# A two-block transformer kernel: the squares of the first input and their sums take a later place in the queues

## The chip, the cores and the metric

The kernel runs on one core of a Trainium2 chip. A core has five engines that run beside each other, each through its own queue in order: TensorE (PE) multiplies matrices into PSUM, VectorE (DVE) and ScalarE (ACT) work element by element, GpSimd (POOL) does small odd jobs, SyncE (SP) issues DMAs. They meet only in semaphores. The metric is the device time of one execution in microseconds (us), less is better; all times below are in us unless marked.

## The reference

One sequence of 512 tokens of width 1024 in float32 goes through two blocks. What the change touches is the beginning of the first:

```python
def rmsnorm(x, g):
    xf = x.astype(jnp.float32)
    y = xf * lax.rsqrt(jnp.mean(xf * xf, axis=-1, keepdims=True) + EPS)
    return (y * g.astype(jnp.float32)).astype(x.dtype)

xn = rmsnorm(h, norm_mix_g[l])
proj = xn @ w_in[l]
p = proj[..., :POOL_WIDTH]                       # 512 columns
uv = jax.nn.gelu(proj[..., POOL_WIDTH:], approximate=False)
u, v = uv[..., :SGU_WIDTH], uv[..., SGU_WIDTH:]  # 512 each
y_pool = pool_mixer(p, pool_w[l], pool_scale[l])
y_sgu = sgu_mixer(u, v, sgu_g[l], sgu_w[l], sgu_b[l])
h = h + jnp.concatenate([y_pool, y_sgu], axis=-1) @ w_out[l]
```

The rest of the first block is an attention over 256 memory tokens and a gated feed-forward with a convolution over three tokens. The second block has a strictly causal stick-breaking attention of 8 heads beside a depthwise convolution of 31 taps, and another such feed-forward:

```python
mask = s_idx < t_idx
log_beta = jax.nn.log_sigmoid(z)
log_one_minus = jnp.where(mask, jax.nn.log_sigmoid(-z), 0.0)
tail = lax.cumsum(log_one_minus, axis=3, reverse=True) - log_one_minus
weights = jnp.where(mask, jnp.exp(log_beta + tail), 0.0)
outs.append(jnp.einsum("bhqk,bkhd->bqhd", weights, vb))
```

## The kernel before

**Number format.** A float32 product is made of three matmuls (`mm3`, L122 to L125): each operand is split into a rounded upper part and a remainder (hi and lo), and hi x hi, hi x lo and lo x hi are added up in PSUM.

**Weights.** They come in units of 1 MB. `prep()` (L174) takes one: SyncE loads it into `raw`, ACT rounds it into `whi` (L195), DVE makes the remainder `wlo` (L196). Each of the three has two buffers. Unit 0 is loaded and rounded in five pieces (1, 1, 2, 2 and 2 eighths), in turn with the chunks of the input x (`load_x`), so that PE can begin early; later units are one piece. Ahead of each piece's rounding stands `first()`: it scales the x chunk with the norm's gain into `B` (ACT, L139) and the remainder `C` (DVE, L140). The norm's 1/rms is not in these: it is a number per token and is multiplied in behind the matmuls.

**The mean of squares.** `Stats.add` takes two chunks of x at a time: ACT squares them into a buffer t4 (L292; there are three of these buffers, shared with other work), DVE adds the halves into `acc` (L300 for the first pair, L303 and L304 for the others). `mean()` multiplies `acc` with ones on PE (L317, groups of four with one column each), POOL takes the power -1/2 (L325), giving `rc`, with one number per token. `spread()` makes from it a row for every partition: DVE L333, PE L336, ACT L338, giving `rb`.

**The first stage.** Units 0 and 1 (`sta_unit`, 48 matmuls each, into the PSUM pairs pp_190 and pp_279) make the pool mixer's 512 columns with the features on the partitions; DVE evacuates them times `rb` (L372), and the windowed sums follow. Then `mov_stage` makes v with the tokens on the partitions, from units 274 and 352 into the pairs pp_349 (tokens 0 to 255) and pp_350 (256 to 511), and ACT evacuates them by a Gelu with `rc` as its scale (L418). The PSUM pool has three pairs.

**Stick-breaking attention.** Per head pair and block of keys, scores z are made on PE (L774, L779), ACT does Abs, Exp and Ln (L782 to L784), DVE a maximum and sum (L785), giving log(1 - beta). It is split into hi (ACT, L131) and lo (DVE, L132), multiplied with -1 matrices on PE for the running sums (L798, L801), and ACT's Exp (L803) gives the weights, which are multiplied with v (L813). The convolution's taps (DVE, L832) are put between.

**What sets the order.** The program is written in one order, but each engine's queue is laid out by the tile framework's scheduler, which goes by a model of its own of each instruction's duration. `tc.issue_after(inst)` keeps what it wraps from being laid out before that instruction. As the scheduler is one pass over all the program, a constraint at the start can move instructions at a later place too.

Of the kernel before, what the change touches and what calls it, by code (L numbers as in the profile page):

```python
# [10 lines left out]
F32 = mybir.dt.float32  # L11
F32R = mybir.dt.float32r
AF = mybir.ActivationFunctionType
ALU = mybir.AluOpType
# [61 lines left out]
def block_kernel(  # L76
# [12 lines left out]
    pe, act, dve, pool, sp = nc.tensor, nc.scalar, nc.vector, nc.gpsimd, nc.sync  # L89
# [55 lines left out]
    def slot(name, dt=F32R, cols=2048):  # L145
        return slots.tile([P, cols], dt, tag=name, name=name)
# [18 lines left out]
    def whole(name, dt=F32R):  # L165
        return Chunks([slot(name + "0", dt), slot(name + "1", dt)])
# [5 lines left out]
    state = {"next": 0, "ready": [], "bank": 0}  # L172

    def prep(pieces=((0, 8),), before=None, between=None, early=None, slots=None):  # L174

        i = state["next"] if early is None else len(PLAN) + early
        if i == len(PLAN) and early is None:
            return
        if early is None:
            state["next"] += 1  # L180
        _, kind, place = (PLAN + EARLY)[i]
        n = place[2] * 256 if kind == "dwn" else UNIT
        raw = wp.tile([P, UNIT], F32, tag="raw", name="raw")
        hi = slot(slots[0]) if slots else wp.tile([P, UNIT], F32R, tag="whi", name="whi")
        lo = slot(slots[1]) if slots else wp.tile([P, UNIT], F32R, tag="wlo", name="wlo")
        for a, b in pieces:
            cs = slice(a * n // 8, b * n // 8)
            if before:
                before(a, b)
            sp.dma_start(out=raw[:, cs], in_=wts[i][:, cs])  # L190
        for a, b in pieces:
            cs = slice(a * n // 8, b * n // 8)
            if between:
                between(a, b)
            act.copy(hi[:, cs], raw[:, cs])  # L195
            dve.tensor_tensor(lo[:, cs], raw[:, cs], hi[:, cs].bitcast(F32), ALU.subtract)  # L196
        if kind == "hlf":
            views = tuple(w.rearrange("p (k j m) -> p k j m", k=4, j=4) for w in (hi, lo))
        elif kind == "mov":
            views = tuple(w.rearrange("p (k n) -> p k n", k=4) for w in (hi, lo))  # L200
        else:
            views = tuple(w[:, :n].rearrange("p (k j m) -> p k j m", j=2, m=P) for w in (hi, lo))
        if early is None:
            state["ready"].append(views)
        return views

    def weights():
        while len(state["ready"]) < 2 and state["next"] < len(PLAN):
            prep()
        return state["ready"].pop(0)  # L210
# [35 lines left out]
    h = whole("A", F32)  # L246
# [97 lines left out]
    st = Stats(eng=dve)  # L344

    def first(a, b):
        for j in range(a, b):
            scale_split(xh[:, j, :], xl[:, j, :], h[:, j, :], par("g_mix", j))

    prep(PIECES, load_x, first)  # L350
    sp.dma_start(out=sm[:, NFIRST:], in_=small[:, NFIRST:])
    prep()
    memr = half("D0", KC, M, F32)
    sp.dma_start(out=memr, in_=memT.rearrange("(c p) t -> p c t", p=P))
# [2 lines left out]
    sp.dma_start(out=sgw, in_=sguw.rearrange("s (h t) -> s h t", h=4))  # L357
    sp.dma_start(out=plw, in_=poolw.rearrange("c (g d) -> c g d", g=4))
    sp.dma_start(out=sgb, in_=sgub.rearrange("o (h t) -> o h t", h=4).to_broadcast([P, 4, P]))
    for c in range(4):  # L360
        st.add(h[:, 2 * c : 2 * c + 2, :], last=c == 3)

    dh, dl = half("E0", 4, T), half("E1", 4, T)
    for u in range(2):
# [119 lines left out]
    def residual(xh, xl, nxt_h, nxt_l, g, nk=KC):  # L484

        st = Stats()
        for u in range(4):
            pt = sta_unit(xh, xl, nk)
            hu = h[:, 2 * u : 2 * u + 2, :]
            dve.tensor_tensor(hu, pt, hu, ALU.add)  # L490
            for c in (2 * u, 2 * u + 1):
                scale_split(nxt_h[:, c, :], nxt_l[:, c, :], h[:, c, :], par(g, c))
            st.add(hu, last=u == 3)
        return st

    x2h, x2l = whole("F"), whole("G")
    st = residual(yh, yl, x2h, x2l, "g_x")
# [96 lines left out]
    st = residual(oh, ol, x3h, x3l, "g_ffn")  # L594
# [386 lines left out]
    st = Stats()  # L981
# [121 lines left out]
```

## Time and profile before

| | |
|---|---|
| median of 3 runs | 1246.66 (1246.56 to 1247.7) |
| profiled execution | 1246.8 |
| its span | 1245.1 |
| PE busy | 1226.2 (98%) |
| DVE busy | 771.2 (62%) |
| ACT busy | 485.2 (39%) |
| POOL busy | 110.0 (9%) |
| HBM read and written | 117.45 MB, 94 GB/s over the span |

The profiled execution is 0.14 above the median. A row of the timeline has the start, the length, the engine, the line of the kernel, the operation with what it writes and reads, the shapes and the count of neighbours taken together; in brackets stands the idle time of the engine before it and what ended it. Matmul lengths overlap: one of 512 columns is shown with 0.39, and the next one starts 0.227 later.

### The profile page before, as it was taken

What the parts mean: (1) busy time and instruction counts of PE and PEld (TensorE: products, weight loads), DVE (VectorE), ACT (ScalarE), POOL (GpSimd) and SP (SyncE); (2) the same over time, 40 slices, a digit from 0 to 9 for tenths busy, and PEclk for the clock granted to TensorE, in tenths of its full rate; (3) what the DMA queues carried; (4) which work ended last, traced back from release to release, by engine and by line L of the source; (5) the groups of instructions that cost most, each with busy time, mean ns of one, the idle gap of its engine ahead of it and who ended that gap; (6) DMA issues with size and microseconds to landing.
All of it is one profiled execution on the core that took longest, in us unless ns stands there. A gap on an engine that the chain in (4) does not pass through costs nothing.

```text
span 1245.1 us, 13634 instructions
## 1 busy us (share of the span) xinstructions
PE 1226.2 (98%) x5712; PEld 1009.9 (81%) x5712; DVE 771.2 (62%) x813; ACT 485.2 (39%) x528; POOL 110.0 (9%) x125
## 2 busy tenths in 40 slices
PE   8999999999999999999999899999999999999998
PEld 6889888788888888888888778677888888888887
DVE  7855634744766664466375999985775555346532
ACT  6433424623544342243254125873443333223310
POOL 1100210012000000000054412000400000000000
PEclk9999999999999999999999999999999999999999
DMA  8233332312222222222343012201222233223222
GB/s 275 97 106 131 102 102 68 136 68 101 74 97 102 102 102 102 92 83 97 118 152 135 0 35 68 68 1 68 102 99 81 92 102 102 102 102 102 84 68 86
DMA packets 20445, 118.32 MB, mean 95 GB/s; under 512 B 2208, under 2 KB 4128, under 8 KB 7712
## 3 DMA queue, kind: packets, MB, share of 16 engines
q1 hardware_dynamic: 20096, 117.20, 27.4%
q8 instruction: 44, 0.72, 0.2%
q10 hardware_dynamic: 288, 0.26, 0.1%
q14 instruction: 17, 0.14, 0.0%
HBM read 115.35 MB, written 2.10 MB: 94 GB/s over the span
## 4 chain that ended last, share of the span: by engine, by line
PE 92%; DVE 4%; ACT 2%; issue 1%; POOL 1%; DMA 0%; SPq 0%; DVEq 0%; ACTq 0%
PE pp L125 28%; PE pp L123 28%; PE pp L124 28%; DVE H L832 2%; PE ps L123 1%; PE ps L124 1%; PE ps L125 1%; POOL col L739 0%; PE ps L317 0%; DMA A<-in_xT 0%; PE ps L813 0%; DVE t L785 0%; PE pp L774 0%; ACT t L783 0%; PE pp L745 0%
## 5 line engine op out<-in xcount | busy, mean ns | idle before, releaser
L195 ACT CAST whi<-raw 128x2048 fp32r<-128x2048 f32 (+3 forms) x109 | 197.9, 1817 | 425.7 <-PE pp L124 358.5
L196 DVE TENSOR_TENSOR wlo<-raw,whi 128x2048 fp32r<-128x2048 f32 (+3 forms) x109 | 236.7, 2173 | 71.3 <-ACT whi L195 70.7
L123 PE MATMUL pp<-B,whi 128*128 128x512 f32 x672 | 261.7, 390 | 2.4 <-ACT whi L195 2.4
L125 PE MATMUL pp<-B,wlo 128*128 128x512 f32 x672 | 262.1, 390 | 0.2
L124 PE MATMUL pp<-C,whi 128*128 128x512 f32 x672 | 261.8, 390 | 0.0
L124 PE MATMUL pp<-G,whi 128*128 128x512 f32 x448 | 175.1, 391 | 0.0
L125 PE MATMUL pp<-F,wlo 128*128 128x512 f32 x416 | 162.2, 390 | 0.0
L123 PE MATMUL pp<-F,whi 128*128 128x512 f32 x416 | 161.5, 389 | 0.0
L123 PEld LDWEIGHTS pp<-B,whi 128*128 128x128 f32 x672 | 126.2, 188 | 29.3 <-ACT whi L195 3.3
L125 PEld LDWEIGHTS pp<-B,wlo 128*128 128x128 f32 x672 | 126.1, 188 | 27.8 <-DVE wlo L196 1.5
L124 PEld LDWEIGHTS pp<-C,whi 128*128 128x128 f32 x672 | 126.2, 188 | 26.7 <-issue 0.5
L124 PEld LDWEIGHTS pp<-G,whi 128*128 128x128 f32 x448 | 84.1, 188 | 17.6 <-issue 0.2
L625 DVE TENSOR_TENSOR A<-pp,A 128x1024 f32<-128x1024 f32 x23 | 28.2, 1224 | 105.6 <-PE pp L125 105.6
L646 DVE SCALAR_TENSOR_TENSOR H<-H,sm,H 128x512 f32<-128x512 f32 x132 | 92.8, 746 | 0.7
L125 PEld LDWEIGHTS pp<-F,wlo 128*128 128x128 f32 x416 | 78.1, 188 | 16.4 <-issue 0.2
L123 PEld LDWEIGHTS pp<-F,whi 128*128 128x128 f32 x416 | 78.1, 188 | 16.4 <-issue 0.2
L832 DVE SCALAR_TENSOR_TENSOR H<-H,sm,H 128x512 f32<-128x512 f32 x120 | 90.2, 780 | 1.2
L651 DVE TENSOR_TENSOR H<-pp,rb 128x1024 f32<-128x1024 f32 x22 | 26.8, 1224 | 50.6 <-PE pp L125 44.4
L128 ACT ACTIVATE H<-H,sm 128x512 f32<-128x512 f32 x70 | 54.3, 808 | 7.5 <-DVE H L698 7.5
L997 DVE TENSOR_TENSOR H<-pp,rb 128x512 f32<-128x512 f32 x22 | 15.2, 691 | 60.9 <-PE pp L125 54.7
L123 PE MATMUL pp<-D,whi 128*128 128x512 f32 x112 | 43.6, 389 | 0.0
L124 PE MATMUL pp<-E,whi 128*128 128x512 f32 x112 | 43.6, 389 | 0.0
(293 smaller groups left out, 1797.9 us busy)
## 6 DMA issues: line engine op xcount, KB each, us to landing
raw<-in_wts SPq DMA_DIRECT2D x99, 1024.0 KB, 4.8
raw<-in_wts SPq DMA_DIRECT2D x8, 768.0 KB, 4.0
A<-in_xT SPq DMA_DIRECT2D x3, 512.0 KB, 6.8
out<-A SPq DMA_DIRECT2D x3, 512.0 KB, 2.8
D<-in_memT SPq DMA_DIRECT2D x1, 1024.0 KB, 10.7
raw<-in_wts SPq DMA_DIRECT2D x3, 256.0 KB, 7.0
A<-in_xT SPq DMA_DIRECT2D x2, 256.0 KB, 3.9
raw<-in_wts SPq DMA_DIRECT2D x2, 128.0 KB, 4.1
```

What stands on the lines that cost most here:

```text
L123: pe.matmul(out, wh, xh, start=start, stop=False, **kw)
L124: pe.matmul(out, wh, xl, start=False, stop=False, **kw)
L125: pe.matmul(out, wl, xh, start=False, stop=stop, **kw)
L128: act.activation(out, in_, AF.Identity, scale=scale, bias=bias)
L195: act.copy(hi[:, cs], raw[:, cs])
L196: dve.tensor_tensor(lo[:, cs], raw[:, cs], hi[:, cs].bitcast(F32), ALU.subtract)
L625: dve.tensor_tensor(hu, pt, hu, ALU.add)
L646: dve.scalar_tensor_tensor(dst, hs[:, k : k + 512], w(k), dst, ALU.mult, ALU.add)
L651: dve.tensor_tensor(hs[:, :, 2:], pt, over2(rb), ALU.mult)
L832: tap = dve.scalar_tensor_tensor(cv[:, i, :], cc[:, i, k : k + 512], par("dw_w", 4 * k + i), cv[:, i, :], ALU.mult, ALU.add)
L997: dve.tensor_tensor(hs[:, 2:514], pt[:, 0, :], rb, ALU.mult)
```

## The change

`prep()` remembers its last rounding and its last remainder. All four calls of `st.add` are wrapped, so that nothing of them is laid out before the last rounding of unit 0 (`first_hi`) nor before the remainder of unit 1 (`state["lo"]`, the latest `prep()` at that place). No instruction is added or removed. Behind the change the line numbers are up by 3.

```diff
--- before.py
+++ after.py
@@ -192,8 +192,8 @@
             cs = slice(a * n // 8, b * n // 8)
             if between:
                 between(a, b)
-            act.copy(hi[:, cs], raw[:, cs])
-            dve.tensor_tensor(lo[:, cs], raw[:, cs], hi[:, cs].bitcast(F32), ALU.subtract)
+            state["hi"] = act.copy(hi[:, cs], raw[:, cs])
+            state["lo"] = dve.tensor_tensor(lo[:, cs], raw[:, cs], hi[:, cs].bitcast(F32), ALU.subtract)
         if kind == "hlf":
             views = tuple(w.rearrange("p (k j m) -> p k j m", k=4, j=4) for w in (hi, lo))
         elif kind == "mov":
@@ -348,6 +348,7 @@
             scale_split(xh[:, j, :], xl[:, j, :], h[:, j, :], par("g_mix", j))
 
     prep(PIECES, load_x, first)
+    first_hi = state["hi"]
     sp.dma_start(out=sm[:, NFIRST:], in_=small[:, NFIRST:])
     prep()
     memr = half("D0", KC, M, F32)
@@ -357,8 +358,10 @@
     sp.dma_start(out=sgw, in_=sguw.rearrange("s (h t) -> s h t", h=4))
     sp.dma_start(out=plw, in_=poolw.rearrange("c (g d) -> c g d", g=4))
     sp.dma_start(out=sgb, in_=sgub.rearrange("o (h t) -> o h t", h=4).to_broadcast([P, 4, P]))
+
     for c in range(4):
-        st.add(h[:, 2 * c : 2 * c + 2, :], last=c == 3)
+        with tc.issue_after(first_hi.ins), tc.issue_after(state["lo"].ins):
+            st.add(h[:, 2 * c : 2 * c + 2, :], last=c == 3)
 
     dh, dl = half("E0", 4, T), half("E1", 4, T)
     for u in range(2):
```

Where it goes, by the queues. First ACT in the first stage, before: `t4_*` are the squares, `whi_121` is unit 0, `whi_161` unit 1, `B` and `A` the scaled and the plain input.

```order
L195 CAST whi_121<-raw_120 128x512
L139 ACTIVATE B1_117<-A1_77,sm_73 128x512 x2
L292 ACTIVATE t4_180<-A1_77 128x1024
L195 CAST whi_121<-raw_120 128x512
L139 ACTIVATE B1_117<-A1_77,sm_73 128x512 x2
L292 ACTIVATE t4_184<-A1_77 128x1024
L195 CAST whi_121<-raw_120 128x512
L195 CAST whi_161<-raw_160 128x2048
L139 ACTIVATE H0_462<-D0_166,sm_73 128x256 x8
```

and in the changed kernel:

```order
L195 CAST whi_121<-raw_120 128x512
L139 ACTIVATE B1_117<-A1_77,sm_73 128x512 x2
L195 CAST whi_121<-raw_120 128x512
L292 ACTIVATE t4_172<-A0_76 128x1024
L292 ACTIVATE t4_176<-A0_76 128x1024
L292 ACTIVATE t4_180<-A1_77 128x1024
L195 CAST whi_161<-raw_160 128x2048
L139 ACTIVATE H0_462<-D0_166,sm_73 128x256 x8
L131 CAST G1_461<-G0_168 128x512 x2
L292 ACTIVATE t4_184<-A1_77 128x1024
L195 CAST whi_274<-raw_273 128x2048
L195 CAST whi_352<-raw_351 128x2048
L421 ACTIVATE F0_459<-pp_349,rc1_246 128x512 x2
```

Every square has left unit 0; three stand as a block ahead of unit 1's rounding, the fourth behind the memory's scaling (H0) and before unit 274's. The Gelu of pp_349 now stands ahead of the copy of `rb`.

Next PE in the first stage, as a difference: `acc_174` are the summed squares, pp_279 is unit 1's product, pp_349 and pp_350 the two token tiles.

```order
-L317 MATMUL ps0_239<-ones_83,acc_174 128x1 x4
 L125 MATMUL pp_279<-B0_116,wlo_162 128x512
...
-L336 MATMUL ps1_250<-t2_248,ones_83 128x512
 L124 MATMUL pp_279<-C1_119,whi_161 128x512
...
+L125 MATMUL pp_349<-whi_274,C0_118 128x512
+L317 MATMUL ps0_239<-ones_83,acc_174 128x1 x4
+L123 MATMUL pp_349<-whi_352,B1_117 128x512
...
+L336 MATMUL ps1_250<-t2_248,ones_83 128x512
 L123 MATMUL pp_350<-whi_274,B0_116 128x512
```

The sums' matmuls go from the front of unit 1 into the middle of pp_349, the spread from the end of unit 1 to between pp_349 and pp_350, and these two, mixed before, now stand one after the other; pp_350 takes the buffer of pp_349.

Then ACT in the last round of the stick-breaking attention, before (t4_5448, t4_5485 and t4_5542 are three blocks of scores; C0_5228, B0_5267 and D1_5095 their rounded logarithms; C1 and E1 weights):

```order
L783 ACTIVATE t4_5448<-t4_5448 128x1024
L803 ACTIVATE C1_5243<-pp_5358 128x768
L784 ACTIVATE t4_5448<-t4_5448 128x1024
L803 ACTIVATE E1_5282<-pp_5423 128x768
L782 ACTIVATE t4_5485<-pp_5468 128x768
L131 CAST C0_5228<-t4_5448 128x1024
L783 ACTIVATE t4_5485<-t4_5485 128x768
L784 ACTIVATE t4_5485<-t4_5485 128x768
L782 ACTIVATE t4_5542<-pp_5533 128x768
L783 ACTIVATE t4_5542<-t4_5542 128x768
L784 ACTIVATE t4_5542<-t4_5542 128x768
L131 CAST B0_5267<-t4_5485 128x768
```

and in the changed kernel:

```order
L786 ACTIVATE t4_5448<-t4_5448 128x1024
L787 ACTIVATE t4_5448<-t4_5448 128x1024
L806 ACTIVATE C1_5243<-pp_5358 128x768
L131 CAST C0_5228<-t4_5448 128x1024
L806 ACTIVATE E1_5282<-pp_5423 128x768
L785 ACTIVATE t4_5485<-pp_5468 128x768
L786 ACTIVATE t4_5485<-t4_5485 128x768
L787 ACTIVATE t4_5485<-t4_5485 128x768
L131 CAST B0_5267<-t4_5485 128x768
L806 ACTIVATE C1_5243<-pp_5439 128x1024
L785 ACTIVATE t4_5542<-pp_5533 128x768
L786 ACTIVATE t4_5542<-t4_5542 128x768
```

The first step (Abs) of t4_5485 has moved behind the cast of C0_5228 and the Exp of E1_5282, and t4_5542 behind the cast of B0_5267. PE and DVE are laid out to match: on DVE four taps instead of one stand between the remainder of C0_5228 and t4_5485. SyncE's queue is the same.

## Rows read from the trace of the kernel before

**Rows 1.** The page's first line: each engine's busy time.

```profile
PE 1226.2 (98%) x5712; PEld 1009.9 (81%) x5712; DVE 771.2 (62%) x813; ACT 485.2 (39%) x528; POOL 110.0 (9%) x125
```

**Rows 2.** Busy time by windows of the span, granted clock and DMA share, three stretches.

```profile
5.88:21.14 15.26, 12.60 (x51) 8.81 (x50) 12.71 (x21) 13.28 (x20) 0.82 (x2) 1.00 1.03 374
...
33.83:55.62 21.79, 21.79 (x97) 18.02 (x96) 18.29 (x27) 9.19 (x10) 2.13 (x3) 1.00 0.29 97
813.50:841.60 28.10, 26.46 (x157) 18.95 (x156) 21.99 (x29) 19.43 (x24) 0.00 (x0) 1.00 0.00 1
```

**Rows 3.** PE timeline of the first stage: start, length, group, idle before.

```profile
12.02 0.50 PE L123 MATMUL pp<-B,whi 128*128 128x512 f32 x1 [0.71 <-ACT whi L195]
...
21.59 0.95 PE L317 MATMUL ps<-ones,acc 128*128 128x1 f32 x8
22.41 0.47 PE L125 MATMUL pp<-B,wlo 128*128 128x512 f32 x1
...
31.16 1.02 PE L336 MATMUL ps<-t,ones 128*128 128x512 f32 x2
```

**Rows 4.** ACT timeline of the first stage.

```profile
9.18 1.33 ACT L139 ACTIVATE B<-A,sm 128x512 fp32r<-128x512 f32 x2
...
11.36 0.60 ACT L195 CAST whi<-raw 128x512 fp32r<-128x512 f32 x1
...
15.81 1.04 ACT L292 ACTIVATE t<-A 128x1024 f32<-128x1024 f32 x1
16.76 2.42 ACT L195 CAST whi<-raw 128x512 fp32r<-128x512 f32 x2
...
54.46 2.63 ACT L418 ACTIVATE F<-pp,rc 128x512 f32<-128x512 f32 x4
```

**Rows 5.** DVE timeline of the first stage.

```profile
19.81 2.29 DVE L196 TENSOR_TENSOR wlo<-raw,whi 128x2048 fp32r<-128x2048 f32 x1
...
32.83 1.22 DVE L372 TENSOR_TENSOR t<-pp,rb 128x1024 f32<-128x1024 f32 x1 [3.12 <-ACT rb L338]
```

**Rows 6.** SyncE's DMA issues of an x chunk and of unit 1.

```profile
3.12 0.44 SPq L249 DMA_DIRECT2D A<-in_xT  x1
...
7.68 0.65 SPq L190 DMA_DIRECT2D raw<-in_wts  x1
```

**Rows 7.** DMA landings of those two issues, us after the issue.

```profile
A<-in_xT SPq DMA_DIRECT2D x1, 512.0 KB, 5.8
...
raw<-in_wts SPq DMA_DIRECT2D x1, 1024.0 KB, 9.0
```

**Rows 8.** ACT timeline of the last attention round.

```profile
814.24 0.80 ACT L803 ACTIVATE E<-pp 128x768 f32<-128x768 f32 x1
815.05 0.81 ACT L782 ACTIVATE t<-pp 128x768 f32<-128x768 f32 x1
815.86 1.05 ACT L131 CAST C<-t 128x1024 fp32r<-128x1024 f32 x1
...
820.89 0.81 ACT L131 CAST B<-t 128x768 fp32r<-128x768 f32 x1
```

**Rows 9.** DVE timeline of the last attention round.

```profile
814.61 1.22 DVE L785 SCALAR_TENSOR_TENSOR t<-pp,t 128x1024 f32<-128x1024 f32 x1
...
819.78 0.95 DVE L785 SCALAR_TENSOR_TENSOR t<-pp,t 128x768 f32<-128x768 f32 x1
```

**Rows 10.** Conv taps on DVE in the last attention round, grouped.

```profile
L832 DVE SCALAR_TENSOR_TENSOR H<-H,sm,H x17: 739/745/753, 810.2 to 830.7; 128x512 f32<-128x512 f32 x17
```

**Rows 11.** PE timeline of the last attention round.

```profile
818.20 0.44 PE L801 MATMUL pp<-C,negtri 128*128 128x512 f32 x1
819.25 0.50 PE L801 MATMUL pp<-C,negtri 128*128 128x512 f32 x1 [0.61 <-DVE C L132]
...
821.76 0.33 PE L798 MATMUL pp<-B,negone 128*128 128x128 f32 x1 [0.72 <-ACT B L131]
...
841.59 1.08 PE L813 MATMUL ps<-B,E 128*64 128x512 f32 x4
```

## The prediction

> **What bounds the kernel now.** I read the page first: TensorE (PE) is busy 1226.2 of 1245.1 us [rows 1], so an edit counts only where PE stands still, or is made to. The windows come next, since the share is a mean over stages. From 5.88 to 21.14 us PE is busy 12.60 of 15.26; from 33.83 to 55.62 without a break, 97 matmuls, so one follows another by 0.227; from 813.50 to 841.60, the last round of the second block's attention, 26.46 of 28.10 [rows 2]. The granted clock is 1.00 (the 2.4 GHz level) in all three, so PE's waits there cost their own length and no slower matmuls afterwards. Then the timelines of PE, ACT and DVE in these stretches, and last the DMA landings, which say how early anything can start.
>
> What the reader is to see at the start: unit 0 comes in pieces, and PE waits for ACT's rounding of a piece, 0.71 at 12.02 for the third [rows 3]. On ACT a square of 1.04 stands ahead of the rounding of each piece but the first (the last of the four at 15.81) [rows 4]. That is the loss the edit goes at.
>
> The profiled run took 1246.8, its span 1245.1, so 1.7 lie around the span; the median is 1246.66. I sum on the span and carry the difference to the median.
>
> **Unit 0: -1.48.** Without squares a piece's rounding waits only for its x chunks. For the third piece they are issued at 3.12 and land 5.8 later, at 8.92 [rows 6, 7]. B's two halves take 1.33, the cast 0.60 [rows 4]: ready by 10.8, against 12.02 now. 36 matmuls follow: 36 x 0.227 = 8.2, plus lower parts not yet there. Now these add 21.14 - 12.02 - 8.2 = 0.9; DVE is then rid of the sums as well and I take 0.7 (estimate: the first of the restarts stays, half of the rest goes). Unit 0 ends at 10.8 + 8.2 + 0.7 = 19.66 against 21.14. The fourth and fifth roundings are ready at 12.7 and 14.7, ahead of their matmuls.
>
> **Unit 1: +0.90, so that only -0.58 of it is left.** All squares that a buffer is free for (three) now stand ahead of unit 1's rounding, one block: 14.71 + 3 x 0.945 (start to start) = 17.54. Raw unit 1 was issued at 7.68 and landed 9.0 later, at 16.7 [rows 6, 7], so the rounding starts 0.84 after it could. The rounding and piece 4's together take 2.42, 0.51 of it piece 4's [rows 4]: it ends at 19.45 (before: 19.18). The lower part takes 2.29 [rows 5]: 21.78. PE reaches the first matmul that reads it, the third of unit 1, at 19.66 + 0.45 = 20.11, and goes on at 21.83. Before, that matmul ran at 22.41, behind the column sums. So 1.48 shrinks to 22.41 - 21.83 = 0.58.
>
> **Column sums: +0.90.** L317 runs from 21.59 and the next matmul at 22.41, itself 0.08 longer than 0.39 [rows 3]: 0.90. Before, it stood in front of the matmul that would have waited for the lower part until 19.81 + 2.29 = 22.10 at least [rows 5], and so was mostly paid by that wait. Now it stands in the middle of pp_349, where nothing is waited for, and its 0.90 is paid in full. The spread (L336) costs the same in either place: 1.02 for two passes [rows 3].
>
> **Token tiles: +0.85.** Before, pp_349 and pp_350 were mixed and both had buffers: pp_190 was evacuated at 32.83 [rows 5]. Now the scale 1/rms comes later, pp_190 and pp_279 are still held, and pp_350 takes pp_349's buffer, when both Gelus of pp_349 have read it. By the terms above pp_349 ends at 44.40. The group of four Gelus at 54.46 takes 2.63 [rows 4]: two take 1.36, 0.05 for starting, so PE goes on at 45.86. L336 fills the wait till 45.12 only: +0.73, and 0.12 for a matmul that starts after a wait (0.50 instead of 0.39 at 12.02 [rows 3]). The Trainium skill, "Perfetto Trace Analysis", section "Optimizing Tensor Performance", wants independent matmul groups to rotate through PSUM banks, so that one is evacuated beside the next one's matmuls. That speaks against this order, and the trace agrees as far as it goes: with two buffers there is no idle time between 33.83 and 55.62 [rows 2]. Where the rule was kept the stage would be 0.85 shorter.
>
> First stage: -0.58 + 0.90 + 0.85 = **+1.2**. The rest lies under matmuls. The fourth square and the deferred sums on DVE come before unit 2's parts, but these are ready at 30.2 (wanted 32.4) and those of whi_352 at 36.7 (wanted 38.7); the pool's evacuation, now behind the Gelu on ACT, is over by 53.5, for a PSUM buffer and a unit wanted at 56.9. Each queue on SP is as it was. If that cover failed, the nearest is the 2 us at 38.7: a DVE queue late by 3 would cost 1. Bounds of the stage: without L317's price and the buffer wait -0.6; with twice the buffer wait +2.0.
>
> **Last attention round: +2.6.** Between 60 and 810 us the order is unchanged, but in the last round the scheduler shifted ACT: t4_5485's Abs/Exp/Ln now stand behind the cast of C0_5228 and behind the Exp of E1_5282. Before, E1's Exp (814.24) and t4_5485's Abs (815.05) ran while DVE made t4_5448 (814.61, 1.22 long), and the cast followed at 815.86 [rows 8, 9]. Now ACT has nothing from 814.4 to 815.87, E1's Exp starts at 816.83 (2.6 later), and Abs, Exp, Ln of t4_5485 end at about 820.3. On DVE four conv taps of 0.745 [rows 10] stand ahead of t4_5485's subtraction, which starts at 821.37 instead of 819.78 [rows 9]; with its 0.95 the cast to B0_5267 starts at 822.36 against 820.89 [rows 8]. PE's waits, walked in its new order with these times: 0.93 (t4_5448's subtraction), 0.19 (C's lower part), 2.03 (B's cast), 0.73 (C1's Exp), 0.86 (t4_5542's subtraction), 0.72 (B1's Exp): 5.46. Those that go, start to start: 819.25 - 818.43 = 0.82, then 0.95 up to 821.76 [rows 11], and two short ones of 0.3 each: 2.4. Of the difference of 3.1 I give 0.5 back, since the new order changes less often between the attention's matmuls and those of the next weight unit, and the first one behind such a change takes up to 0.12 more: 2.6. The last gather (841.59 [rows 11]) would be at 844.2. Nothing behind it waits for ACT or DVE so closely that this is won back. Bounds: if all waits that I put here are hidden and the old ones go, -2.3; if the old restarts stay beside the new waits, +4.5. I take 2.6, since each wait stands on durations of rows at the same tiles.
>
> **Sum.** 1.2 + 2.6 = +3.8: the profiled run at 1250.6, the median at 1250.5.
>
> **Rivals.**
> A: the first stage's +1.2 alone; the shifted tail costs nothing. For it: ACT is busy 19.43 and DVE 21.99 of 28.10 there [rows 2], so both have room. Against: PE follows their chain within 1 us, at 819.25 and 821.76. Time: 1246.66 + 1.2 = 1247.9.
> B, the other side: faster. Unit 0's 1.48 is kept if PE isn't held at the third matmul of unit 1. That decides at 20.11: the lower part has to end before it, which takes a rounding that starts at 16.0, and raw lands at 16.7. And the tail's old waits of 0.82 and 0.95 would have to vanish without new ones, C's cast being ahead of t4_5485's Exp and Ln. Full: -1.48 + 0.90 - 1.77 = -2.4, 1244.3; with no L317 cost 1243.4.
> C: the edit does nothing to see. PE's idle time moves from unit 0 to unit 1, L317 falls into a wait, the tail stays: -0.6 to +0.6, about 1246.6.
> D: the tail costs more, since each late cast holds the next square of the chain: +4.5, together 1252.4.
>
> **Chances.** Forecast (1249.2 to 1251.6) 0.50, D 0.17, A 0.13, C 0.10, B 0.10. What can be told from no change is 0.2%, 2.5 us: slower begins at 1249.2, faster ends at 1244.2. Forecast and D make 0.67 slower, 0.03 of A's cases come out above the line: 0.70. A's and C's rest and B where only its first half comes true: 0.22 within. Faster 0.08. The range, 1247.0 to 1252.8, reaches down to A and up to D and leaves out C and B.
>
> **What would show it.** Right: no wait of PE over 1 us between 8 and 20; unit 0 ends near 19.7; a wait of 1.7 for wlo at the third matmul of unit 1; L317 at about 38.7; a wait of PE for the Gelu (ACT) of 0.7 at 45; the first matmul behind the token tiles 1.2 later, at 56.9; and in the round around 815 to 824 us a wait near 2 for the cast of B. Wrong: unit 1 without a wait, or the last gather of B less than 2 us later against the stage's own start.

## The result: slower, by twice the forecast

The changed kernel takes 1254.38 us (median of 5, 1249.85 to 1255.13) where the kernel before takes 1246.69 (5 runs, 1246.56 to 1247.7): 7.7 more, a ratio of 1.0055 with a 95% interval of 1.0036 to 1.0073. The forecast was 1250.5, in a range up to 1252.8. The direction held, the size didn't.

The page of the changed kernel's profiled run (1254.99) has at its head:

```profile
span 1253.3 us, 13627 instructions
PE 1232.1 (98%) x5712; PEld 1014.8 (81%) x5712; DVE 772.9 (62%) x813; ACT 485.3 (39%) x528; POOL 111.6 (9%) x125
```

The span grew by 8.2, PE's busy time by 5.9 [rows 1], with the same instructions. A wait is not busy time: matmuls have become slower somewhere, and that is the first thing to look for. The mean granted clock of the run is 0.992 (before: 0.997). Four of the five timed runs have 0.992 or 0.993; the fifth, 1249.85, has 0.997.

To see where the time goes I follow six marks that both orders have:

| mark on PE | before | changed | difference |
|---|---|---|---|
| third matmul of unit 1 | 22.41 | 22.23 | -0.18 |
| first matmul behind the token tiles | 55.62 | 57.20 | +1.58 |
| column sums of the last norm (L317 x16) | 666.48 | 668.02 | +1.54 |
| last transposes of the keys (L745, L748) | 759.81 | 762.28 | +2.47 |
| last gather of the attention round | 841.59 | 850.47 | +8.88 |
| last matmul of the program | 1241.05 | 1249.22 | +8.17 |

So there are four steps: +1.6 in the first stage, +0.9 between 668 and 762, where the order is the same, +6.4 in the last attention round (forecast 2.6), and -0.7 after it. The last of them belongs to the round: the queues differ behind it too, up to about 900 us, and the changed one has four of the next norm's column sums (L898, 0.43 at 850.04) ahead of the last gather, where the old one has all eight behind it. So round and rest together cost 5.7.

The first stage, PE of the changed kernel, in the columns of [rows 3]:

```profile
10.70 0.49 PE L123 MATMUL pp<-B,whi 128*128 128x512 f32 x1 [1.55 <-ACT whi L195]
...
22.23 0.50 PE L125 MATMUL pp<-B,wlo 128*128 128x512 f32 x1 [1.59 <-DVE wlo L196]
...
38.24 0.95 PE L317 MATMUL ps<-ones,acc 128*128 128x1 f32 x8
...
44.63 1.02 PE L336 MATMUL ps<-t,ones 128*128 128x512 f32 x2
46.21 0.50 PE L123 MATMUL pp<-whi,B 128*128 128x512 f32 x1 [0.56 <-ACT F L421]
...
57.20 0.39 PE L123 MATMUL pp<-B,whi 128*128 128x512 f32 x1
```

Unit 0 has waits of 1.55 and 0.20, where before it had 1.71 (at 9.33) and 0.71; then come those that were forecast: 1.59 for unit 1's lower part, the sums alone at 38.24, and 0.56 for the Gelu at the token tiles. ACT shows why unit 1 is late, as against [rows 4]:

```profile
13.36 1.34 ACT L139 ACTIVATE B<-A,sm 128x512 fp32r<-128x512 f32 x2 [0.70 <-DMA A<-in_xT]
...
15.11 2.95 ACT L292 ACTIVATE t<-A 128x1024 f32<-128x1024 f32 x3
17.97 1.89 ACT L195 CAST whi<-raw 128x2048 fp32r<-128x2048 f32 x1
...
44.89 1.27 ACT L421 ACTIVATE F<-pp,rc 128x512 f32<-128x512 f32 x2 [10.16 <-PE pp L125]
```

The three squares take 15.11 to 17.97, and unit 1's rounding begins behind them.

The last attention round on PE, to set beside [rows 11]:

```profile
817.04 0.91 PE L777 MATMUL pp<-G,F 64*128 64x256 f32 x12 [0.96 <-ACT C L806]
...
825.70 0.33 PE L801 MATMUL pp<-B,negone 128*128 128x128 f32 x1 [1.15 <-ACT B L131]
826.62 1.44 PE L816 MATMUL ps<-C,E 128*64 128x512 f32 x4 [0.60 <-ACT C L806]
...
834.98 0.80 PE L123 MATMUL pp<-G,whi 128*128 128x512 f32 x1
835.58 0.63 PE L124 MATMUL pp<-G,whi 128*128 128x512 f32 x1
...
837.60 0.39 PE L123 MATMUL pp<-G,whi 128*128 128x512 f32 x1
...
850.47 1.08 PE L816 MATMUL ps<-B,E 128*64 128x512 f32 x4
```

The waits are no longer than the sum had them: 1.15 for B's cast (2.03 in the sum) and 0.60 for C1's second Exp (0.73). The one of 0.96 at 817 is as long as the first in the sum (0.93), but it is another: it ends with ACT's Exp of C1 from pp_5358, which the new order puts behind the Ln of t4_5448, and the sum had the subtraction of t4_5448 on DVE. What the sum did not have is below them. From the gather of four at 826.62 on the matmuls are slow: it takes 1.44 (1.08 at the end of the list, the same operation), and the first matmuls of the next unit stand 0.42 to 0.60 apart where 0.227 is usual. In windows (the columns of [rows 2]; the granted clock is the third number from the end):

```profile
817.00:824.00 7.00, 6.91 (x50) 4.91 (x50) 6.86 (x10) 4.15 (x5) 0.00 (x0) 1.00 0.00 0
824.00:827.00 3.00, 1.25 (x7) 0.68 (x7) 2.96 (x4) 2.18 (x3) 0.00 (x0) 1.00 0.00 0
827.00:838.00 11.00, 10.95 (x43) 7.71 (x40) 7.82 (x11) 8.02 (x10) 0.00 (x0) 0.53 0.00 0
838.00:850.00 12.00, 12.00 (x59) 9.28 (x59) 5.19 (x8) 5.28 (x7) 0.00 (x0) 1.00 0.01 1
```

PE is busy 1.25 of the 3.00 us before 827, and then the granted clock is 0.50, its 1.2 GHz level, from 827.2 to 837.5; after that 1.00 again. In the same round of the kernel before it is 1.00 throughout [rows 2].

### The profile page after: what moved, and what is told of

Its sections match the earlier page's. It is cut to its first block, busy times and chain, and to the rows that moved or that the text cites. A ratio compares the mean times of both kernels' runs of the same rounds, so it can differ in the third digit from the quotient of the medians.

```text
span 1253.3 us, 13627 instructions
## 1 busy us (share of the span) xinstructions
PE 1232.1 (98%) x5712; PEld 1014.8 (81%) x5712; DVE 772.9 (62%) x813; ACT 485.3 (39%) x528; POOL 111.6 (9%) x125
## 4 chain that ended last, share of the span: by engine, by line
PE 91%; DVE 4%; ACT 2%; POOL 1%; DMA 1%; issue 0%; SPq 0%; DVEq 0%; ACTq 0%
PE pp L123 28%; PE pp L124 28%; PE pp L125 28%; DVE H L835 2%; PE ps L123 1%; PE ps L124 1%; PE ps L125 1%; DMA A<-in_xT 1%; PE ps L816 0%; POOL col L742 0%; PE ps L317 0%; PE pp L804 0%; PE pp L777 0%; DVE wlo L196 0%; DVE t L788 0%
```

## The experiments

Two theories and a third, before the first four runs. **Theory 1**: the round's waits were summed rightly, and the rest is the granted clock, which falls because of them. **Theory 2**: the waits themselves cost 6.4. **Theory 3**: the clock falls since the round begins later, whatever its order. To separate stage and round, a table of instructions is put at the end of the program; it holds a stretch of each queue to a given order, by edges that make no wait:

```python
ORDER = ("5477-5484 5523-5528 5534-5541 5505-5520 5565 ...", ...)   # by number as traced
    by = {i.name: i for i in nc.cur_bb.bb.instructions}
...
        for one, two in zip(names, names[1:]):
            tc.add_manual_dep(by[two], one, ..., reason="order")
```

**1. The changed stage, the round as before.** The table holds the round to the order of before.

> The changed first stage with the last attention round in the order of before. Theory 1 (the changed order of the round lets the granted clock fall, and that is most of the missing size): the round keeps 1.00 and takes as long as before; what is left is the first stage's 1.5 and, behind the normalised queries, a low clock that lasts longer (0.9): 1248.2 to 1249.2. Theory 2 (the round's new waits cost 6.4 by themselves, the clock is no cause): the same 1248.2 to 1249.2. Theory 3 (the later arrival at the round, not its order, makes the clock fall): a low clock in the round here too, 1251 or more.

Measured: 1248.83 against 1247.06 (ratio 1.0015, 1.0006 to 1.0024): +1.8. The round, in windows:

```profile
813.00:830.00 17.00, 15.35 (x111) 11.25 (x112) 16.79 (x23) 15.71 (x20) 0.00 (x0) 1.00 0.00 1
830.00:860.00 30.00, 30.00 (x137) 22.58 (x134) 19.16 (x27) 11.88 (x15) 1.01 (x1) 1.00 0.10 36
```

The clock is 1.00 all through, and from the keys' last transposes (761.38) to the last gather (843.19) it takes 81.8, as before (841.59 - 759.81 = 81.8). The round begins nearly as late as in the changed kernel (762.28) and nothing falls: theory 3 is out for the profiled run. Ten of the eleven runs lie between 1247.89 and 1249.58; one of 1250.76 has a mean clock of 0.994 and no trace, so where its clock was low isn't known (run 5 shows a place in the first stage).

**2. The stage as before, the changed round.** The same table the other way round.

> The first stage of before with the last attention round in the order of the changed kernel. Theory 1: some runs, most of them perhaps, with a low clock in the round and 1251 to 1253.5, the others at 1248.5 to 1249.5. Theory 2: 1253 in all runs, whatever the clock. Theory 3: no low clock in the round, about 1249.2 (the 2.6 of waits alone).

Measured: 1252.07 (1250.81 to 1253.99), ratio 1.0042 (1.0029 to 1.0055): +5.0. The profiled run, a stretch of 14 us in the round:

```profile
823.00:837.00 14.00, 13.35 (x46) 9.03 (x47) 9.97 (x12) 9.37 (x11) 0.00 (x0) 0.51 0.00 0
```

Almost the whole stretch is at half speed, though the round begins as early as before. The clock falls at 823.3, which is behind the wait for B's cast and ahead of the next one:

```profile
823.01 0.33 PE L819 MATMUL pp<-B,negone 128*128 128x128 f32 x1 [1.15 <-ACT B L152]
823.93 1.97 PE L834 MATMUL ps<-C,E 128*64 128x512 f32 x4 [0.60 <-ACT C L824]
```

```profile
821.90:823.30 1.40, 0.29 (x1) 0.19 (x1) 1.36 (x3) 1.17 (x2) 0.00 (x0) 1.00 0.00 0
823.40:823.90 0.50, 0.00 (x0) 0.00 (x0) 0.50 (x2) 0.50 (x2) 0.00 (x0) 0.50 0.00 0
```

So in this run the wait of 0.60 was not needed for the fall. In the five runs the mean clock goes from 0.992 (1253.99 and 1253.46) over 0.994 (1252.07 and 1251.31) to 0.995 (1250.81): the time falls as the clock rises, so the price is not one fixed number, which speaks for theory 1 and against 2. The second group that theory 1 had, 1248.5 to 1249.5, did not come.

**3. The waits filled.** The changed kernel, with matmuls in PE's three long waits: four into an idle bank, eleven that add zeros to the gather's sum.

```diff
+        if (hp, n) == (3, 0):
+            idle = single(0).rearrange("p (a b) -> p a b", a=4)
+            for _ in range(4):
+                pe.matmul(idle, negone, over2(negone, 4), start=True, stop=True)
...
+            for _ in range(11 if (hp, n) == (2, 2) else 0):
+                pe.matmul(o[:HD, P:]..., identr[:HD, HD:], negone[:HD]..., start=False, ...)
```

> The changed kernel with TensorE's three long waits in the round filled by matmuls whose results are dropped (4 into an idle PSUM bank) or are zeros added to a sum (11). Theory 1: the granted clock stays 1.00 and the last gather comes some 4 us earlier than in the changed kernel; median 1249.5 to 1251. Theory 2: filling a wait gives nothing back, 1254 to 1255. Theory 3: as theory 2, the clock falls wherever the round begins at that time.

Measured: 1251.29 (1250.42 to 1253.19) against 1247.06, ratio 1.0035 (1.0022 to 1.0047): +4.2, where the changed kernel has +7.7. PE in the round, with the fillers (L796 and L840), and the windows in which the changed kernel waited and was slow:

```profile
815.25 1.09 PE L796 MATMUL ps<-negone 128*128 128x512 f32 x4
...
823.81 1.45 PE L840 MATMUL ps<-negone,identr 64*64 64x384 f32 x7
825.18 0.33 PE L828 MATMUL pp<-B,negone 128*128 128x128 f32 x1
825.44 0.91 PE L840 MATMUL ps<-negone,identr 64*64 64x384 f32 x4
...
846.67 1.08 PE L847 MATMUL ps<-B,E 128*64 128x512 f32 x4
```

```profile
824.00:827.00 3.00, 3.00 (x16) 1.49 (x14) 2.96 (x5) 2.82 (x4) 0.00 (x0) 1.00 0.00 0
827.00:838.00 11.00, 10.03 (x57) 7.44 (x56) 8.96 (x12) 7.52 (x10) 0.00 (x0) 1.00 0.01 1
```

More work, and 3.1 us less time (3.5 by the differences to before, 7.7 and 4.2). The clock stays at 1.00 and the last gather is at 846.67 instead of 850.47. Theory 2 falls, theory 1 stands. And the difference to the first run, 1251.29 - 1248.83 = 2.5, is about what the changed round costs without the clock, where the forecast had 2.6. In the traces it is made up otherwise: from the keys' last transposes (761.61) to the last gather it takes 85.1, 3.3 more than in run 1, and 0.7 comes back behind the gather.

**4. The squares behind unit 1's rounding.** The round is as before. In the changed kernel the constraint on unit 1's remainder, a DVE instruction, shows in the sums on DVE alone: the squares on ACT still stand ahead of unit 1's rounding. Here they are held behind that rounding.

```diff
-        with tc.issue_after(first_hi.ins), tc.issue_after(state["lo"].ins):
+        with tc.issue_after(state["hi"].ins), tc.issue_after(state["lo"].ins):
```

> The squares behind unit 1's rounding instead of ahead of it (their sums behind its lower part as in the changed kernel), the round in the order of before. If the block of three squares ahead of unit 1's rounding is what takes back unit 0's gain, the third matmul of unit 1 runs near 21.0 instead of 22.2, and the first matmul behind the token tiles at 55.9 to 56.3 instead of 57.2: total 0.9 to 1.2 below the run with the changed stage alone. If unit 1's rounding waits for its data anyway, no difference from that run.

Measured: 1247.58, ratio 1.0006 (0.9996 to 1.0015), 1.25 less than run 1. PE of the stage:

```profile
20.69 0.50 PE L146 MATMUL pp<-B,wlo 128*128 128x512 f32 x1 [0.86 <-DVE wlo L217]
...
44.82 0.50 PE L144 MATMUL pp<-whi,B 128*128 128x512 f32 x1 [0.56 <-ACT F L442]
...
55.81 0.39 PE L144 MATMUL pp<-B,whi 128*128 128x512 f32 x1
```

The third matmul of unit 1 is at 20.69 instead of 22.23, and the stage ends at 55.81 instead of 57.20 (57.06 in run 1). The block of squares costs what was expected, 1.25; the 0.56 at the token tiles and the sums' 0.9 remain, and eat the gain.

**5. Which waits?** Run 3 without the four matmuls of the first wait.

> The changed kernel with only the second and the third of the round's three long waits filled (1.15 and 0.60, both after 824), by 11 matmuls that add zeros; the first wait (0.96 at 817) stays empty. If these two make the clock fall, it stays at 1.00 and the time is that of the run with all three filled, 1250.5 to 1251.5 (the changed kernel: 1254.4). If the first wait has a part in it, some runs fall: 1252 to 1254.5.

Measured: 1250.98 (1250.84 to 1252.72), ratio 1.0033 (1.002 to 1.0045): as run 3. The wait of 0.95 at 817.77 is there, the clock in the round is 1.00. So the first wait alone let nothing fall in these runs, and one or both of the waits after 824 matter; by run 2 the first of these can be enough without the second. The profiled run is the one of 1252.72. Its low clock lies from 715 to 725, a stretch that comes up below, and in the first stage, behind the wait for unit 1's lower part:

```profile
21.31 0.50 PE L147 MATMUL pp<-B,wlo 128*128 128x512 f32 x1 [1.59 <-DVE wlo L218]
```

```profile
22.20:25.60 3.40, 3.40 (x10) 2.62 (x9) 3.40 (x10) 3.40 (x5) 0.00 (x0) 0.50 0.96 371
```

The wait of 1.59 is in the changed kernel and in runs 1 and 3 too, and there the clock is 1.00 in this window. Here the stretch from that matmul to the first one behind the token tiles takes 36.58 (to 57.89) and in the changed kernel 34.97: 1.6 more, in one execution of four.

**6. A better stage.** Squares and sums directly behind unit 1's parts, L317 in the middle of unit 1, everything else in the order of before, by a table.

> All four squares and their sums directly behind unit 1's parts, the column sums (L317) in the middle of unit 1, all else in the order of before (the two token tiles mixed, the spread in its old place). Theory 1 (three terms make the stage's 1.6: the block ahead of unit 1's rounding, the sums at full price, the wait for a PSUM pair): without the first and the third, the third matmul of unit 1 runs near 20.9 (before 22.41), the sums cost 0.9, no wait at the token tiles, and the stage ends 0.4 to 0.7 earlier than before: 1246.2 to 1246.8. Rival (the squares cost the same wherever they stand): the stage ends with before or later, 1247.0 and up.

Measured: 1248.58, ratio 1.001 (1.0001 to 1.0019): a miss. PE:

```profile
20.89 0.50 PE L164 MATMUL pp<-B,wlo 128*128 128x512 f32 x1 [0.86 <-DVE wlo L235]
...
26.37 1.05 PE L356 MATMUL ps<-ones,acc 128*128 128x1 f32 x8 [0.65 <-DVE acc L343]
...
55.95 0.39 PE L162 MATMUL pp<-B,whi 128*128 128x512 f32 x1
```

The third matmul of unit 1 comes at 20.89 as expected, and nothing is waited for at the token tiles. But L317 stands too early and waits 0.65 for DVE's sums; with its price the stage ends at 55.95, 0.33 later than before. The other part of the loss, 1.4 in the profiled run, lies between the last norm's sums (666.83) and the keys' last transposes (761.54; before 666.48 and 759.81), in the stretch that the next run is about. The rival's number came out, for another reason than it gave.

**7. The kernel before, its own two longest waits filled.** If a wait costs its length and the slow work behind it, that must hold in the kernel before as well. At 714 PE waits for the normalised queries:

```profile
713.97 1.56 PE L745 MATMUL pp<-ident,D 128*128 128x128 f32 x8 [3.64 <-DVE D L741]
717.62 1.94 PE L745 MATMUL pp<-ident,D 128*128 128x128 f32 x8 [2.08 <-DVE D L741]
719.32 0.80 PE L123 MATMUL pp<-E,B 128*128 128x512 f32 x1
719.91 0.63 PE L124 MATMUL pp<-E,B 128*128 128x512 f32 x1
```

```diff
+            if name == "G":
...
+                for _ in range((15, 10)[i]):
+                    pe.matmul(idle, negone, over2(negone, 4), start=True, stop=True)
```

> The kernel before with the two longest waits of TensorE (3.64 at 710 and 2.08 at 716, for the normalised queries) filled by 15 and 10 matmuls into an idle PSUM bank. Theory 1 (what a wait costs is its length and, where the clock falls, the work behind it at half speed): the clock stays 1.00 between 710 and 725, the transposes behind the first wait take 1.04 instead of 1.56, the matmuls of 717.6 to 721.8 run at full speed: 1.8 to 2.4 less, 1244.7 to 1245.4. Theory 2 (the clock is no cause of lost time): no difference, 1247.0.

Measured: 1245.67 (11 runs, 1245.07 to 1247.81) against 1247.2 (27 runs), ratio 0.9988 (0.9979 to 0.9996): 1.5 less, where 1.8 to 2.4 were expected. PE:

```profile
709.77 3.56 PE L784 MATMUL ps<-negone 128*128 128x512 f32 x15
713.82 1.06 PE L788 MATMUL pp<-ident,D 128*128 128x128 f32 x8 [0.49 <-DVE D L778]
714.63 2.54 PE L784 MATMUL ps<-negone 128*128 128x512 f32 x10
717.47 1.06 PE L788 MATMUL pp<-ident,D 128*128 128x128 f32 x8 [0.29 <-DVE D L778]
719.17 0.50 PE L160 MATMUL pp<-E,B 128*128 128x512 f32 x1 [0.64 <-DVE t L730]
719.51 0.40 PE L161 MATMUL pp<-E,B 128*128 128x512 f32 x1
```

The transposes take 1.06 instead of 1.56 and 1.94, the matmuls behind them are 0.23 to 0.34 apart instead of 0.42 to 0.59. From the last norm's sums to the keys' last transposes this run takes 92.66 (666.08 to 758.74), the profiled run of before 93.33, that of the changed kernel 94.26: 0.7 to 1.6 are won, and not 2: now PE waits 0.64 for DVE at 719.17, which did not show behind the slow transposes.

**8. Runs 6 and 7 together.**

> The two before this together. If they are independent, their differences add up: 2.2 to 3.1 below before, 1244.0 to 1244.9.

Measured: 1246.6, ratio 0.9996 (0.9987 to 1.0005). It is 0.9 above run 7, and 2.0 under run 6. The expected 1244.0 to 1244.9 did not come, since run 6 had no gain to add: its 1.4 lost and run 7's 1.5 won make -0.1, and -0.6 is measured. The fastest version is run 7, 1.5 below the kernel before, where the changed one is 7.7 above it.

## Why the forecast was wrong

**The step that failed** stands in its first part: "The granted clock is 1.00 (the 2.4 GHz level) in all three, so PE's waits there cost their own length and no slower matmuls afterwards." The clock was read in the old order, and taken over into an order with other waits; there it fell to 0.50 from 827.2 to 837.5, a price for which the sum had no term. Runs 1 and 3 give the price: 7.7 = 1.8 (stage, run 1) + 2.5 (the round's waits, run 3 less run 1) + 3.4 (what is left, and what filling the waits takes back: 3.1 to 3.5). The one execution of the changed kernel with a mean clock of 0.997 agrees: it took 1249.85, 3.2 more than before, where the forecast was 3.8. It has no trace. None of the rivals held it; rival D had a larger price of the round, but from waits.

**Unit 0 and unit 1**: right in kind. (The sign that no wait of PE is over 1 us between 8 and 20 did not come: 1.55 at 10.70. But the third piece starts there, as the sum had it, at 10.8.) Unit 1's rounding does stand behind three squares and PE does wait for the lower part; the wait was forecast as 1.7 and is 1.59. The gain that stays was forecast as 0.58 and is 0.18 (22.41 - 22.23): ACT waited for the last x chunks until 13.36 (before, they had landed at 12.95), the squares began at 15.11 and not at 14.71, and unit 1 moved by the same 0.4.

**Column sums** (+0.90) and **token tiles** (+0.85): right. L317 runs at 38.24 (forecast 38.7), PE goes on at 46.21 after a wait of 0.56 and the spread. Stage: -0.18 + 0.90 + 0.85 = 1.57, measured 1.58 in the trace and 1.8 in run 1, forecast 1.2. The order of PE differs between 77 and 90 us as well, where the sum had it unchanged; the marks at 57 and 668 differ by the same 1.5 to 1.6, so that cost nothing.

**The round's waits**: the total fits (2.5 against 2.6), in part by luck. Of the 5.46 of waits, the changed kernel and run 3 show 3.7: 0.96 for an Exp that the sum did not name, 1.15 for B's cast (2.03), 0.60 for C1's Exp (0.73), and in run 3 0.31 for the last subtraction (0.86) and 0.66 for B1's Exp (0.72); none for C's lower part (0.19). And the forecast had 2.6 at the last gather and nothing won back behind it, where run 3 has 3.3 and 0.7. ACT's row of the swapped instructions is as forecast:

```profile
818.34 1.05 ACT L131 CAST C<-t 128x1024 fp32r<-128x1024 f32 x1 [1.35 <-DVE t L788]
819.29 0.81 ACT L806 ACTIVATE E<-pp 128x768 f32<-128x768 f32 x1
...
824.82 0.83 ACT L131 CAST B<-t 128x768 fp32r<-128x768 f32 x1 [2.26 <-DVE t L788]
```

ACT idles 1.35 before C's cast, E1's Exp starts behind it, and 2.26 pass before B's cast.

**Rivals**: A's bare stage is run 1. B, the other side, needed unit 1 without a wait, and the wait of 1.59 is there; even in run 4, with unit 1's third matmul 1.5 earlier, the stage isn't ahead of before. C would have needed the sums to fall into a wait; they don't.

**What wasn't in the sum at all**: +0.9 between 668 and 762. The order there is that of before, and the long wait at 714 is too. The low clock lasted from 714.6 to 724.8 here, in the profiled run of before from 714.4 to 721.2. A window of before that holds it, in the columns of [rows 2]:

```profile
714.00:722.00 8.00, 5.92 (x24) 4.86 (x25) 7.56 (x8) 2.75 (x3) 2.13 (x2) 0.57 0.01 2
```

and one of the changed kernel, 3 us longer and with a lower mean clock:

```profile
714.00:725.00 11.00, 7.77 (x26) 6.43 (x27) 10.41 (x11) 2.75 (x3) 3.52 (x4) 0.53 0.08 13
```

In the profiled runs of kernels whose order is equal there, it is 6.8 us (before, runs 1 to 4) or 10.2 (the changed kernel, runs 5 and 6). In the long ones the clock fell 0.5 to 1.4 us before the transposes behind the longest wait resumed, in the short ones between 0.3 before and 1.5 after. Why it falls at another moment isn't settled; it is no effect of the change that I can show, and it makes up 0.9 of the 8.2 in the spans. The kernel before varies as much by itself: of its 27 runs beside runs 5 to 8, 17 have a mean clock of 0.997 (median 1246.7) and 9 one of 0.996 (median 1247.56).

## What to carry to other kernels

A wait of TensorE has two prices: its length, and, if the granted clock falls, the work behind it at half speed, which can be the larger. That the clock is 1.00 in a stretch of the old profile says so of the old order alone; where a change adds waits close together in a stretch that had some already, put the fall among the rivals with its own price, several us of half-speed matmuls. And an instruction held back at the program's start can make a whole-program scheduler reorder a place 800 us later: compare the whole queue, and give that place a sum of its own.

## What the runs showed of the hardware

In the changed kernel waits of 1.15 and 0.60, with PE busy 1.25 of 3.00 us, were followed by 10.2 us at the 1.2 GHz level, though PE had work nearly all through them; in run 2 the level fell behind the wait of 1.15 and ahead of the one of 0.60, and stayed for 13.7. Behind the longest wait, 3.64 at 710, it lasts 6.8 or 10.2. The length of one wait does not decide it: 1.40 at 808.21 is in the trace of before and, 0.02 longer at most, in all the others, and the clock is 1.00 behind it each time; 1.59 at unit 1's third matmul was followed by a low clock in run 5 and not in three other traces of the same stage. The Trainium skill, "TensorE: Matmul & The Clock Gate", section "HAM oscillation — how this bites in real kernels", tells of waits for DMA, longer than those of the round, after which the next matmuls start at the low clock. The traces agree on the low clock behind idle time; they differ in that waits of about 1 us, and for ACT, were enough in the round. Matmuls with no use in the wait keep the clock: 25 of them take 1.5 us off the kernel before, 11 take 3.4 off the changed one.

DMA landings differ between executions of the same queue: the last x chunks of unit 0 were used at 13.36 in the changed kernel and at 12.62 in run 4, though SyncE issued them at 5.08 there and at 5.49 in run 4, in the same order. A term that rests on one landing carries up to 0.7 us of that.
